# The last down projection of a two-layer trunk with Strassen's products for 8 of its 22 pairs of k-tiles

## The chip, the cores and the metric

The kernel runs on one core of one Trainium2 chip. The metric is the device time of one execution in microseconds (us), as the median over runs. The core's engines run side by side, each through its own queue in order: PE (TensorE, matrix products into PSUM banks), DVE (VectorE), ACT (ScalarE), POOL (GpSimd) and SP (SyncE, which here only issues loads and stores). An instruction that must wait holds up everything behind it in its engine's queue.

## The reference, cut to what matters

```python
for l in range(DEPTH):                     # DEPTH = 2, SEQ = 256 tokens, D_MODEL = 2048
    h = rmsnorm(x, g_mix[l])
    ...                                    # attention, spatial gating, merge
    x = x + merged @ w_out[l]
    x = x + conv_ffn(rmsnorm(x, g_ffn[l]), w_up[l], conv_w[l], conv_b[l], w_down[l])
return rmsnorm(x, g_final)

def conv_ffn(h, w_up, conv_w, conv_b, w_down):
    a, b = jnp.split(h @ w_up, 2, axis=-1)
    ...                                    # causal depthwise convolution of a
    return (jax.nn.gelu(acc) * b) @ w_down # (256 x 5632) @ (5632 x 2048)
```

All is float32. The change concerns the very last product, `(gelu(acc) * b) @ w_down[1]`, and the final norm behind it.

## The kernel before

Every float32 product with a weight matrix is made of three passes: each operand is split into two float32r parts, hi and lo, and hi\*hi, hi\*lo and lo\*hi are accumulated in PSUM. The weights arrive as tiles of two k-tiles (2 x 128 rows of the matrix) by 512 columns, `raw`, 512 KB each, loaded by SP (`fetch`, L98) into a ring of 5 buffers. `split_w` makes `hi` (ACT, L108) and `lo = raw - hi` (DVE, L109), into rings of 3 buffers each; `raw` is free for the next load when `lo` is made, and `hi` and `lo` are free when PE has used them.

In the last down projection the tokens lie on the partitions: there are NT = 2 token tiles t, FT/2 = 22 pairs m of k-tiles, and NB = 4 column blocks n of 512. The operand of pair m is `gT[m]` (two k-tiles, hi and lo, 256 tokens), in one of the 30 buffers of the `arena`. `rows` takes one column block at a time: for each of 22 pairs it loads and splits one raw tile and issues 12 matmuls of 512 columns (2 k-tiles x 2 token tiles x 3 passes; L117 to L119) into the two banks of one accumulator (`acc_banks`, ring of 3 tiles of 2 banks; two more single banks, `tp_bank`, serve the transposes). So the stage is 4 x 22 x 12 = 1056 matmuls of 512 columns. In the last column block `late=4` puts the first token tile of the last four pairs ahead of the second, so that its end runs under PE's work on the second.

Ahead of the stage the residual stream `xT` (features on partitions, 8 tiles in `xpool`) is transposed by PE through the two `tp` banks (L597, four transposes to a bank) and copied by DVE (L598) into `xb`. After each column block DVE adds the product to `xb` (L607), ACT squares and sums (L609), POOL multiplies by the gain (L611). At the end comes the norm (L613 to L619) and the four blocks are scaled and stored (L623 to L628).

The order of the instructions on each engine is set by the framework's scheduler when the program is built, which also adds the waits between engines. Nothing of it is written by hand in this stage. A tile's ring buffer is handed to the tile that comes next in that order.

Of the kernel before, what the change touches and what calls it, by code (L numbers as in the profile page):

```python
# [9 lines left out]
F32 = mybir.dt.float32  # L10
# [7 lines left out]
P = 128  # L18
# [23 lines left out]
def trunk_kernel(ctx, tc, x, g_mix, w_in, b_forget, g_sgu, w_spatial, b_spatial,  # L42
                 w_branch_a, w_branch_b, w_out, g_ffn, w_up, conv_w, conv_b,
                 w_down, g_final, out):
    """Every float32 product with a weight matrix runs as three float32r passes: each operand is
    the exact sum of two parts of 12 significant bits, hi and lo, and hi*hi + hi*lo + lo*hi
    is accumulated in PSUM. The RMS factor of a token is applied to the products, since it is
    one number per token; the gain goes into the transposed operand."""
# [95 lines left out]
    def cols_(w2d, c0, ops):  # L144
        """Products with features on the partitions, 512 features: two of [feature, f, half, token],
        where the sum of the two halves is the product."""
# [25 lines left out]
    def gained(src, gains):  # L172
        """[feature, 2, token] times a gain per feature, as an operand."""
        op = operand()
        for j in range(2):
            a = nc.scalar.activation(op[:, j, 0, :], src[:, j, :], AF.Identity, scale=gains[:, j:j + 1])
        for j in range(2):
            v = nc.vector.scalar_tensor_tensor(op[:, j, 1, :], src[:, j, :], gains[:, j:j + 1],
                                           op[:, j, 0, :].bitcast(F32), op0=ALU.mult, op1=ALU.subtract)
        return op, (a, v)  # L180
# [13 lines left out]
    def inv_rms(sq):  # L194
        """Sums of squares by feature -> [P, NT] by token, 1/sqrt(mean + eps)."""
# [9 lines left out]
    def spread(inv):  # L205
        """[P, NT] by token -> [P, 2, T], the same on every partition and twice."""
# [8 lines left out]
    def params(l):  # L215
        """Gains, conv weights and forget bias; gain() and rest() lay them out with channels on partitions."""
# [40 lines left out]
    def sgu_weights(raw):  # L257
        """The lower triangles of the spatial weights, transposed."""
# [31 lines left out]
    # ---- the first loads and products: x is transposed ahead of the chunk that needs it; until it  # L290
    # is there, products of ones keep the tensor engine's clock up ----
# [49 lines left out]
    for l in range(DEPTH):  # L341
# [191 lines left out]
        def residual(w2d, ops, sq, gains):  # L533
            """xT += w2d^T ops; its squares; its product with the gains as operands."""
# [57 lines left out]
    xb = [unit([NT, 512]) for _ in range(NB)]  # L592
    for m in range(KT // 2):
# [4 lines left out]
        nc.vector.tensor_copy(xb[m // 2][:, :, m % 2 * T:m % 2 * T + T], tp.rearrange("p (t c) -> p t c", t=NT))  # L598
    ss = small.tile([P, NT, NB], F32, tag="ss", name=nm("ss"))
    fin = small.tile([P, NT], F32, tag="fin", name=nm("fin"))  # L600
    for n in range(NB):
        gf = scratch([P, 512])
        nc.gpsimd.dma_start(gf, g_final[None, n * 512:(n + 1) * 512].broadcast_to([P, 512]))
        acc = rows(w_down[DEPTH - 1], n * 512, 512, gT, late=4 if n == NB - 1 else 0)
        for t in range(NT):
            z = xb[n][:, t, :]
            nc.vector.tensor_tensor(z, acc[t], z, op=ALU.add)  # L607
            junk = scratch([P, 512])
            nc.scalar.activation(junk, z, AF.Square, accum_out=ss[:, t, n:n + 1])  # L609
            if n < NB - 1:  # L610
                nc.gpsimd.tensor_tensor(z, z, gf, op=ALU.mult)  # L611
        if n == NB - 2:
            nc.vector.tensor_reduce(fin, ss[:, :, 0:NB - 1], axis=AX.X, op=ALU.add)  # L613
            nc.vector.tensor_scalar(fin, fin, 1.0 / D, EPS, op0=ALU.mult, op1=ALU.add)
    for t in range(NT):
        f_ = fin[:, t:t + 1]
        z = xb[NB - 1][:, t, :]
        nc.vector.scalar_tensor_tensor(f_, ss[:, t, NB - 1:NB], 1.0 / D, f_, op0=ALU.mult, op1=ALU.add)
        nc.gpsimd.tensor_tensor(f_, f_, mhalf[:, 0:1], op=ALU.pow)  # L619
        nc.vector.tensor_tensor(z, z, gf, op=ALU.mult)  # L620
# [37 lines left out]
```

## Time and profile before

| what | value |
|---|---|
| runs, median of 3 (lowest to highest) | 2717.92 us (2717.62 to 2718.63) |
| span of the profiled execution | 2717.0 us |
| median less that span, taken as what lies around it | 0.9 us |
| PE busy, DVE busy, ACT busy, POOL busy | 2702.2, 1640.7, 1304.5, 521.8 us |
| first matmul of the stage, last matmul of the program | at 2465.63 and 2707.51 us |
| share of the DMA engines' time, 2520 to 2580 us | 0.62, at 198 GB/s |

Times inside the profile count from the span's start. A row of groups gives the line of the kernel, engine, operation, the tiles (out<-in), shapes and count, then busy time in us and the mean of one in ns, then the engine's idle time before them and what ended it. A row of the timeline begins with start and length in us; for DVE the length reaches past the start of the next instruction, so the distance of starts, not the length, is the pace. "DMA to landing" runs from the issue of a load by SP to its arrival.

### The profile page before, as it was taken

What the parts mean: (1) busy time and instruction counts of PE and PEld (TensorE: products, weight loads), DVE (VectorE), ACT (ScalarE), POOL (GpSimd) and SP (SyncE); (2) the same over time, 40 slices, a digit from 0 to 9 for tenths busy, and PEclk for the clock granted to TensorE, in tenths of its full rate; (3) what the DMA queues carried; (4) which work ended last, traced back from release to release, by engine and by line L of the source; (5) the groups of instructions that cost most, each with busy time, mean ns of one, the idle gap of its engine ahead of it and who ended that gap; (6) DMA issues with size and microseconds to landing.
All of it is one profiled execution on the core that took longest, in us unless ns stands there. A gap on an engine that the chain in (4) does not pass through costs nothing.

```text
span 2717.0 us, 38197 instructions
## 1 busy us (share of the span) xinstructions
PE 2702.2 (99%) x15120; PEld 2348.1 (86%) x15120; DVE 1640.7 (60%) x1748; ACT 1304.5 (48%) x1581; POOL 521.8 (19%) x414
## 2 busy tenths in 40 slices
PE   9999999999999999999999999999999999999998
PEld 7988888888888888888889888888888888888887
DVE  5555665666666666555555556555667676766444
ACT  5454555554444444444444545555444444444443
POOL 2200113312222222100002011133122222221000
PEclk9999999999999999999999999999999999999999
DMA  7566556656666666656665655566566666665664
GB/s 233 163 198 179 170 164 186 187 187 193 182 193 184 194 180 197 204 190 190 188 185 157 201 175 173 169 188 187 190 183 188 188 189 187 188 189 190 197 198 154
DMA packets 268219, 505.13 MB, mean 186 GB/s; under 512 B 16216, under 2 KB 33032, under 8 KB 268040
## 3 DMA queue, kind: packets, MB, share of 16 engines
q1 hardware_dynamic: 267144, 500.59, 60.8%
q8 instruction: 118, 1.93, 0.3%
q0 software_dynamic: 320, 1.05, 0.1%
q10 hardware_dynamic: 576, 1.05, 0.1%
q14 instruction: 61, 0.50, 0.1%
HBM read 500.53 MB, written 2.10 MB: 185 GB/s over the span
## 4 chain that ended last, share of the span: by engine, by line
PE 97%; POOL 1%; issue 0%; DMA 0%; ACT 0%; DVE 0%; SPq 0%; POOLq 0%; ACTq 0%
PE acc L158 54%; PE acc L160 27%; PE acc L118 4%; PE acc L117 4%; PE acc L119 4%; PE tp L119 1%; PE tp L117 1%; PE tp L118 1%; POOL sq L188 0%; POOL u L170 0%; PE tp L469 0%; PE tp L490 0%; DMA u<-in_x_dram 0%; POOL tmp L420 0%; PE tp L412 0%
## 5 line engine op out<-in xcount | busy, mean ns | idle before, releaser
L158 PE MATMUL acc<-u,hi 128*128 128x512 f32 x6336 | 2206.5, 396 | 0.0
L109 DVE TENSOR_TENSOR lo<-raw,hi 128x1024 fp32r<-128x1024 f32 (+2 forms) x959 | 1239.7, 1297 | 1013.8 <-ACT hi L108 1011.6
L160 PE MATMUL acc<-u,lo 128*128 128x256 f32 x6336 | 1738.9, 280 | 0.0
L108 ACT CAST hi<-raw 128x1024 fp32r<-128x1024 f32 (+2 forms) x959 | 992.4, 1036 | 1203.5 <-PE acc L158 934.4
L158 PEld LDWEIGHTS acc<-u,hi 128*128 128x128 f32 x6336 | 1175.3, 188 | 260.8
L160 PEld LDWEIGHTS acc<-u,lo 128*128 128x128 f32 x6336 | 1193.5, 188 | 20.9 <-issue 0.4
L118 PE MATMUL acc<-lo,u 128*128 128x512 f32 (+1 forms) x584 | 217.7, 373 | 0.9 <-DVE lo L109 0.9
L117 PE MATMUL acc<-hi,u 128*128 128x512 f32 (+1 forms) x584 | 215.7, 369 | 0.0
L119 PE MATMUL acc<-hi,u 128*128 128x512 f32 (+1 forms) x584 | 215.1, 368 | 0.0
L564 POOL TENSOR_TENSOR tmp<-tmp,bc 128x512 f32<-128x512 f32 x44 | 56.4, 1281 | 376.7 <-DVE tmp L166 351.8
L118 PEld LDWEIGHTS acc<-lo,u 128*128 128x128 f32 x584 | 110.3, 189 | 16.6 <-DVE lo L109 1.5
L117 PEld LDWEIGHTS acc<-hi,u 128*128 128x128 f32 x584 | 110.3, 189 | 15.7
L119 PEld LDWEIGHTS acc<-hi,u 128*128 128x128 f32 x584 | 110.3, 189 | 15.2
L571 DVE SCALAR_TENSOR_TENSOR tmp<-tmp,cv,tmp 128x256 f32<-128x256 f32 x176 | 118.5, 721 | 0.0
L170 POOL TENSOR_TENSOR u<-tmp,u 128x512 fp32r<-128x512 f32 x68 | 110.4, 1626 | 39.5 <-ACT u L169 39.5
L188 POOL TENSOR_TENSOR sq<-sq,tmp 128x512 f32<-128x512 f32 x28 | 40.6, 1451 | 400.8 <-ACT tmp L187 399.7
L165 ACT COPY tmp<-acc 128x512 f32<-128x512 f32 x160 | 93.4, 584 | 40.0 <-PE acc L160 40.0
L166 DVE TENSOR_TENSOR tmp<-acc,tmp 128x512 f32<-128x512 f32 x160 | 109.0, 682 | 2.1 <-ACT tmp L165 0.9
L574 POOL TENSOR_TENSOR tmp<-tmp,bc 128x512 f32<-128x512 f32 x44 | 76.3, 1734 | 119.0 <-ACT tmp L573 119.0
L503 POOL TENSOR_TENSOR tmp<-tmp,bc 128x512 f32<-128x512 f32 x32 | 41.5, 1297 | 284.6 <-DVE tmp L166 284.6
L580 POOL TENSOR_TENSOR tmp<-tmp,tmp 128x512 f32<-128x512 f32 x44 | 57.0, 1296 | 190.4 <-DVE tmp L166 164.4
L169 ACT CAST u<-tmp 128x512 fp32r<-128x512 f32 x68 | 42.0, 620 | 43.6 <-POOL tmp L528 35.7
(165 smaller groups left out, 880.2 us busy)
## 6 DMA issues: line engine op xcount, KB each, us to landing
raw<-in_w_up_dram SPq DMA_DIRECT2D x352, 512.0 KB, 4.5
raw<-in_w_in_dram SPq DMA_DIRECT2D x255, 512.0 KB, 3.8
raw<-in_w_down_dram SPq DMA_DIRECT2D x176, 512.0 KB, 4.6
raw<-in_w_out_dram SPq DMA_DIRECT2D x64, 512.0 KB, 4.7
raw<-in_w_in_dram SPq DMA_DIRECT2D x48, 344.0 KB, 3.1
raw<-in_w_branch_b_dram SPq DMA_DIRECT2D x32, 512.0 KB, 4.7
raw<-in_w_branch_a_dram SPq DMA_DIRECT2D x32, 512.0 KB, 4.3
u<-in_x_dram SPq DMA_DIRECT2D x8, 256.0 KB, 7.3
```

Of the source, the lines that this page charges most:

```text
L108: a = nc.scalar.copy(hi, raw)
L109: v = nc.vector.tensor_tensor(lo, raw, hi.bitcast(F32), op=ALU.subtract)
L117: m0 = nc.tensor.matmul(o, lhsT=op[:, j, 0, ts], rhs=hi[:, jw, :], start=start, stop=False)
L118: nc.tensor.matmul(o, lhsT=op[:, j, 0, ts], rhs=lo[:, jw, :], start=False, stop=False)
L119: nc.tensor.matmul(o, lhsT=op[:, j, 1, ts], rhs=hi[:, jw, :], start=False, stop=stop)
L158: nc.tensor.matmul(acc[i][:, f, :], lhsT=hi[:, j, fs], rhs=xhl, start=k == 0, stop=False, skip_group_check=True)
L160: nc.tensor.matmul(acc[i][:, f, T:2 * T], lhsT=lo[:, j, fs], rhs=xh, start=False, stop=k == nk - 1, skip_group_check=True)
L165: nc.scalar.copy(dst, a[:, :, 1, :])
L166: nc.vector.tensor_tensor(dst, a[:, :, 0, :], dst, op=ALU.add)
L170: eng.tensor_tensor(op[:, :, 1, :], src, op[:, :, 0, :].bitcast(F32), op=ALU.subtract)
L571: nc.vector.scalar_tensor_tensor(y[:, f, :], a[:, f, tap:tap + T], cv[:, tap, ft:ft + 1], y[:, f, :], op0=ALU.mult, op1=ALU.add)
L574: nc.gpsimd.tensor_tensor(y, y, inv_b, op=ALU.mult)
```

## The change

The column blocks are now taken two at a time (g = 0, 1; q = 0, 1 inside), all eight PSUM banks are used as accumulators at once, and for 8 of the 22 pairs (m = 3, 5, ... 17) the 2 x 2 x 2 block product (2 token tiles, 2 k-tiles, 2 column blocks) is formed by 7 block products in place of 8, in Winograd's form of Strassen's algorithm. For such a pair DVE forms four sums of weight blocks (L687, L688, L692, L693), three of them in place in the two raw tiles `ra` and `rb`, and four splits follow in place of two: of `ra`, of `rb` after its sum, of `ra` after its sums, and of the half-size sum `t1` (L702 on ACT, L703 on DVE). The four sums of operand blocks are made once per pair, in g = 0 (`sums`: five additions on POOL, L610 to L614, the split on ACT L615 and DVE L616), kept in four arena buffers and in the eight `xpool` tiles, and used again in g = 1. In g = 0 the eight pairs stand at places 3, 5, ... 17 of 22, in g = 1 at places 0, 2, ... 14, each followed by a plain pair. After the last of them in a group, the products P1, R7, R6 and R5 are combined and added to `xb` (L707 to L716), beside the remaining plain pairs. P2, R3, Q4 and E are the banks of the four results (token tile, block): a plain pair adds to them (`plain`), now token tile by token tile with both blocks inside. At the end LATE = 2 pairs take the place of the four late chunks.

```diff
+    def sums(m, hi, lo):
+        z, s_ = scratch([P, 2, T]), scratch([P, 4, P])
+        nc.gpsimd.tensor_tensor(z, gT[m][:, :, 0, :].bitcast(F32), gT[m][:, :, 1, :].bitcast(F32), op=ALU.add)
+        nc.gpsimd.tensor_tensor(s_[:, 0, :], z[:, 0, P:T], z[:, 1, P:T], op=ALU.subtract)
...
+        nc.scalar.copy(hi, s_)
+        nc.vector.tensor_tensor(lo, s_, hi.bitcast(F32), op=ALU.subtract)
...
-    for n in range(NB):
-        gf = scratch([P, 512])
-        nc.gpsimd.dma_start(gf, g_final[None, n * 512:(n + 1) * 512].broadcast_to([P, 512]))
-        acc = rows(w_down[DEPTH - 1], n * 512, 512, gT, late=4 if n == NB - 1 else 0)
+    for g in range(NB // 2):
...
+        b0, b1, b2 = (acc_banks() for _ in range(3))
+        bank = {"P1": b0[:, 0], "P2": b0[:, 1], "R7": b1[:, 0], "R3": b1[:, 1], "R6": b2[:, 0], "R5": b2[:, 1],
+                "Q4": tp_bank(), "E": tp_bank()}
...
+        for i, m in enumerate(order):
+            A = left(m)
+            ra, rb = (fetch(w2d, 2 * m, 2, (n0 + q) * 512, 512) for q in range(2))
+            if i not in paired:
...
+                for t in range(1 if late else NT):
+                    plain(A, ws, t, i == NG - 1)
+                continue
...
+            t1 = scratch([P, 512])
+            nc.vector.tensor_tensor(t1, ra[:, 0, :], rb[:, 0, :], op=ALU.add)
+            nc.vector.tensor_tensor(rb[:, 0, :], rb[:, 0, :], rb[:, 1, :], op=ALU.add)
+            hi, lo = split_w(ra)
+            go("P1", A[0, 0], hi[:, 0, :], lo[:, 0, :], i == lastS)
+            go("P2", A[0, 1], hi[:, 1, :], lo[:, 1, :])
+            nc.vector.tensor_tensor(ra[:, 0, :], ra[:, 0, :], rb[:, 0, :], op=ALU.add)
+            nc.vector.tensor_tensor(ra[:, 1, :], ra[:, 1, :], ra[:, 0, :], op=ALU.add)
+            hi, lo = split_w(rb)
+            go("R7", s_[3], hi[:, 0, :], lo[:, 0, :], i == lastS)
+            go("R3", s_[4], hi[:, 1, :], lo[:, 1, :])
+            hi, lo = split_w(ra)
+            go("R6", s_[2], hi[:, 0, :], lo[:, 0, :], i == lastS)
+            go("Q4", A[1, 1], hi[:, 1, :], lo[:, 1, :])
...
+            nc.scalar.copy(hi, t1)
+            nc.vector.tensor_tensor(lo, t1, hi.bitcast(F32), op=ALU.subtract)
+            go("R5", s_[1], hi, lo, i == lastS)
```

In what follows the lines L599 to L747 are those of the changed kernel; L599 and L600 are its L597 and L598.

The first place is DVE at the start of the stage, before the change. `lo` are the splits of w_down's tiles in the order of the loads, L166 belongs to the last up projection, and the copies empty the transposes' banks.

```order
L109 TENSOR_TENSOR lo_21772<-raw_21769,hi_21771 128x1024
L166 TENSOR_TENSOR tmp_21680<-acc_21502,tmp_21680 128x512
L109 TENSOR_TENSOR lo_21790<-raw_21787,hi_21789 128x1024
L166 TENSOR_TENSOR tmp_21687<-acc_21503,tmp_21687 128x512
L109 TENSOR_TENSOR lo_21808<-raw_21805,hi_21807 128x1024
L598 COPY u_21694<-tp_21698 128x2x256
L598 COPY u_21694<-tp_21704 128x2x256
L109 TENSOR_TENSOR lo_21826<-raw_21823,hi_21825 128x1024
```

The same place now; raw_21877 and raw_21879 are the seventh and eighth loads of w_down, those of the first Strassen pair.

```order
L109 TENSOR_TENSOR lo_21810<-raw_21805,hi_21809 128x1024
L166 TENSOR_TENSOR tmp_21687<-acc_21503,tmp_21687 128x512
L687 TENSOR_TENSOR tmp_21890<-raw_21877,raw_21879 128x512
L600 COPY u_21694<-tp_21698 128x2x256
L600 COPY u_21694<-tp_21704 128x2x256
L688 TENSOR_TENSOR raw_21879<-raw_21879 128x512
L600 COPY u_21695<-tp_21710 128x2x256
L600 COPY u_21695<-tp_21716 128x2x256
L600 COPY u_21696<-tp_21722 128x2x256
L600 COPY u_21696<-tp_21728 128x2x256
L600 COPY u_21697<-tp_21734 128x2x256
L616 TENSOR_TENSOR u_21746<-tmp_21882,u_21746 128x512
```

The first sum of weights has moved ahead of all eight copies, and the copies have moved together ahead of the fourth split of w_down.

The second place is DVE inside g = 1, one Strassen pair with the plain pair that follows it in the order of places. Before the change there are only splits there, and two additions at the end of a column block:

```order
L109 TENSOR_TENSOR lo_22568<-raw_22565,hi_22567 128x1024
L109 TENSOR_TENSOR lo_22586<-raw_22583,hi_22585 128x1024
L607 TENSOR_TENSOR u_21695<-acc_22157,u_21695 128x512 x2
L109 TENSOR_TENSOR lo_22604<-raw_22601,hi_22603 128x1024
L109 TENSOR_TENSOR lo_22622<-raw_22619,hi_22621 128x1024
```

Now (raw_23044 and raw_23046 are the plain pair, raw_23080 and raw_23082 the `ra` and `rb` of the next Strassen pair, lo_23018 the split of the `rb` before):

```order
L109 TENSOR_TENSOR lo_23018<-raw_23000,hi_23017 128x1024
L109 TENSOR_TENSOR lo_23028<-raw_22998,hi_23027 128x1024
L703 TENSOR_TENSOR lo_23038<-tmp_23002,hi_23037 128x512
L687 TENSOR_TENSOR tmp_23084<-raw_23080,raw_23082 128x512
L109 TENSOR_TENSOR lo_23049<-raw_23044,hi_23048 128x1024
L688 TENSOR_TENSOR raw_23082<-raw_23082 128x512
L109 TENSOR_TENSOR lo_23053<-raw_23046,hi_23052 128x1024
L109 TENSOR_TENSOR lo_23088<-raw_23080,hi_23087 128x1024
L692 TENSOR_TENSOR raw_23080<-raw_23080,raw_23082 128x512
L693 TENSOR_TENSOR raw_23080<-raw_23080 128x512
L109 TENSOR_TENSOR lo_23100<-raw_23082,hi_23099 128x1024
```

The sum L687 of the next Strassen pair stands ahead of both splits of the plain pair before it.

The third place is PE at the start of the stage. Before, the transposes stand in twos between the products:

```order
L117 MATMUL acc_21750<-hi_21807,u_18109 128x512
L597 MATMUL tp_21710<-ident,x_84 128x128 x4
L597 MATMUL tp_21716<-ident,x_85 128x128 x4
L118 MATMUL acc_21750<-lo_21808,u_18109 128x512
L119 MATMUL acc_21750<-hi_21807,u_18109 128x512
```

Now they stand together, after the first 18 products of the stage; acc_21764 is the tile of P1 and P2, tp_21767 is Q4:

```order
L635 MATMUL acc_21764<-lo_21810,u_17711 128x512
L635 MATMUL acc_21764<-hi_21809,u_17711 128x512
L599 MATMUL tp_21710<-ident,x_84 128x128 x4
L599 MATMUL tp_21716<-ident,x_85 128x128 x4
L599 MATMUL tp_21722<-ident,x_86 128x128 x4
L599 MATMUL tp_21728<-ident,x_87 128x128 x4
L599 MATMUL tp_21734<-ident,x_88 128x128 x4
L599 MATMUL tp_21740<-ident,x_89 128x128 x4
L635 MATMUL tp_21767<-hi_21773,u_17704 128x512
```

Q4 and E lie in the transposes' two banks, so their first products come after the last transposes.

More of the change, by code (lines that the diff above doesn't have):

```diff
@@ new lines, in trunk_kernel, with three @@
+    NG = FT // 2
+    NS = 8
+    LATE = 2
+    S = []
+    for i in range(NS):
+        if i < 4:
+            u_ = unit([2, 4, P], F32R)
+            hi, lo = u_[:, 0], u_[:, 1]
+        else:
+            hi, lo = (xpool.tile([P, 4, P], F32R, tag=f"x{2 * (i - 4) + q}", name=nm("sx")) for q in range(2))
+        S.append((hi, lo))
+    of = {i: 3 + 2 * i for i in range(NS)}
+    Sx = {}
+    def three(bank, started, A, hi, lo, last):
+        for q, (l_, r_) in enumerate(((A[0], hi), (A[0], lo), (A[1], hi))):
+            nc.tensor.matmul(bank, lhsT=l_, rhs=r_, start=q == 0 and not started, stop=last and q == 2)
@@ L616, in trunk_kernel @@
         f_ = fin[:, t:t + 1]
-        z = xb[NB - 1][:, t, :]
-        nc.vector.scalar_tensor_tensor(f_, ss[:, t, NB - 1:NB], 1.0 / D, f_, op0=ALU.mult, op1=ALU.add)
+        for n in (2, 3):
+            nc.vector.scalar_tensor_tensor(f_, ss[:, t, n:n + 1], 1.0 / D, f_, op0=ALU.mult, op1=ALU.add)
         nc.gpsimd.tensor_tensor(f_, f_, mhalf[:, 0:1], op=ALU.pow)
-        nc.vector.tensor_tensor(z, z, gf, op=ALU.mult)
+        for q in range(2):
+            z = xb[2 + q][:, t, :]
+            nc.vector.tensor_tensor(z, z, gf[q], op=ALU.mult)
         for n in range(NB):
```

74 lines of the change are left out of this document (66 added, 8 removed).

## The prediction

> **What bounds the kernel now.** I read the page first, then the last 250 us by windows, by groups, by waits and by the timeline of each engine.
>
> ```profile
> PE 2702.2 (99%) x15120; PEld 2348.1 (86%) x15120; DVE 1640.7 (60%) x1748; ACT 1304.5 (48%) x1581; POOL 521.8 (19%) x414
> ...
> PE 97%; POOL 1%; issue 0%; DMA 0%; ACT 0%; DVE 0%; SPq 0%; POOLq 0%; ACTq 0%
> ```
>
> PE is the chain from end to end. A window in the stage says the same (PE, PEld, DVE, ACT, POOL busy, granted clock, DMA share, GB/s): no gap, full clock, DVE half idle.
>
> ```profile
> 2520.00:2580.00 60.00, 60.00 (x266) 49.67 (x266) 28.99 (x24) 24.44 (x26) 3.59 (x3) 1.00 0.62 198
> ```
>
> The paces, from PE's and DVE's timelines:
>
> ```profile
> 2559.95 0.39 PE L119 MATMUL acc<-hi,u 128*128 128x512 f32 x1
> 2560.63 0.39 PE L119 MATMUL acc<-hi,u 128*128 128x512 f32 x1
> 2690.20 2.36 DVE L109 TENSOR_TENSOR lo<-raw,hi 128x1024 fp32r<-128x1024 f32 x2
> 2471.37 1.27 DVE L598 COPY u<-tp 128x512 f32<-128x512 f32 x2
> 2476.13 1.03 PE L597 MATMUL tp<-ident,x 128*128 128x128 f32 x8
> ```
>
> Three matmuls lie between the first two rows: 0.227 us each. The groups below give one split 1.23 us undisturbed (1226 ns) and one copy 0.68; two follow each other in 2.36 and 1.27, so splits start 1.13 apart and half-size operations 0.59. A transpose takes 0.13. The groups from 2440 us to the end (busy us, mean ns | idle before):
>
> ```profile
> L108 ACT CAST hi<-raw 128x1024 fp32r<-128x1024 f32 x93 | 97.9, 1054 | 140.3 <-PE acc L119 106.9 <-PE tp L119 19.8 <-PE acc L158 9.6
> L598 DVE COPY u<-tp 128x512 f32<-128x512 f32 x8 | 5.1, 681 | 0.4 <-PE tp L597 0.4
> L609 ACT ACTIVATE tmp<-u 128x512 f32<-128x512 f32 x8 | 5.0, 624 | 9.9 <-DVE u L607 9.9
> L580 POOL TENSOR_TENSOR tmp<-tmp,tmp 128x512 f32<-128x512 f32 x2 | 2.6, 1293 | 9.7 <-DVE tmp L166 9.7
> L109 DVE TENSOR_TENSOR u<-raw,u 128x1024 fp32r<-128x1024 f32 x2 | 2.5, 1226 | 3.7 <-ACT u L108 3.7
> L620 DVE TENSOR_TENSOR u<-u,tmp 128x512 f32<-128x512 f32 x2 | 1.4, 690 | 0.0
> L614 DVE TENSOR_SCALAR fin<-fin 128x2 f32<-128x2 f32 x1 | 1.1, 1070 | 0.0
> ```
>
> ACT waits for PE, that is for a free `hi`: splits run three tiles ahead. L620 is the nearest row to a sum of weights: an addition of two 128x512 tiles in SBUF, 0.69 us, so 0.59 from start to start. The loads, by SP's own waits and by the line of the load from 2480 to 2690 us:
>
> ```profile
> SPq L98 <- DVE lo L109: 185.8, 82, 3.2
> DMA to landing us min/median/max: 3.6/4.5/4.9
> ```
>
> A load is issued when DVE has made a `lo` and so freed a raw tile, and lands 4.5 us later. That hides now, since five raw tiles stand 2.72 us of PE work apart.
>
> **What is removed.** 8 pairs x 2 groups x 3 matmuls = 48 of 1056 matmuls: 48 x 0.227 = 10.9 us of PE. A Strassen pair and a plain one take 45 x 0.227 = 10.2 us of PE, two plain ones 10.9. The loads stay 88 of 512 KB.
>
> **What is added to engines that are not PE.** DVE: 64 sums (0.59), 16 splits (1.13), 16 half splits L703 and 8 L616 (0.59): 70 us in a stage of 240, of which DVE leaves half idle. By busy time it fits. ACT: 16 casts of 1.05 and 24 of about 0.62, 32 us beside its 140 idle: nothing, as long as PE and DVE are not behind it. POOL: `sums` is off the path after the first two; a 128x128 addition has no row, 0.32 (a quarter of 1.3 for 128x512) to 1.0; I take 0.5, and the high end would add up to 4 us at the start (four rows of 0.5 more for each of two pairs), where ACT's L615 stands ahead of the fourth cast. The combining (L707 to L716) lies beside four or seven plain pairs. The tail after the last matmul keeps its length: the extra L735 and L739 precede the last square. What costs is the order in DVE's queue, at three places.
>
> **Place 1, the start.** Its rows: the first matmul of the stage, the eighth load of w_down, and the landings of the window 2450 to 2480 us.
>
> ```profile
> 2465.63 0.40 PE L117 MATMUL acc<-hi,u 128*128 128x512 f32 x1
> ...
> 2468.35 0.37 SPq L98 DMA_DIRECT2D raw<-in_w_down_dram  x1
> DMA to landing us min/median/max: 4.8/5.7/5.9
> ```
>
> The first L687 needs the seventh and eighth loads. The eighth is issued after the third split, as before at 2468.35, and lands at 2473.15 with 4.8 (bounds 3.6 from the stage and 5.9). DVE sits at L687 from 2468.9. PE starts the stage at 2465.63 and has 18 products, until 2469.7; the next transpose needs a copy that stands behind L687. L687 ends at 2473.8, the first copy at 2474.4, and then copy, L688, two copies in turn at 0.6; from the fifth copy on each pair waits also for PE's transposes of that pair (0.7): the seventh ends at 2479.2, and only then is Q4's bank free. PE is idle 2479.2 - 2469.7 less 24 x 0.13 of transposes that it has to make anyway: 6.4 us (5.2 to 7.5). Late next is the split of the fourth tile, which PE reaches 18 products (4.1 us) later; I count nothing for it.
>
> **Place 2, each Strassen pair after the first two.** The order in g = 1 makes a ring: when the split of `rb` ends, its raw tile goes to the next pair's `rb`; the load takes L; the next L687 waits for it; behind it in the queue stand the two splits of the plain pair, for which PE waits. From one end of `rb`'s split to the next: issue and waking 0.1, L, L687 0.59, split 1.13, L688 0.59, two splits 2.26, L692 and L693 1.18, split 1.23: 7.1 + L. PE needs 10.2. The wait per period is L - 3.1. In g = 0 one L693 goes behind the split and one L616 comes in, the same sum. L: by the stage's rows 3.6 to 4.9, median 4.5; the loads of the ring stand further apart than 2.72 us, so I take 4.3, a little under the median. 1.2 x 13 periods (7 in g = 0, 6 in g = 1) = 15.6 us; by the bounds 0.5 x 13 = 6.5 and 1.8 x 13 = 23.4.
>
> [...]
>
> In g = 0 POOL's additions run beside DVE. Two rows of DVE and POOL at the start of the stage:
>
> ```profile
> 2469.70 1.75 DVE L109 TENSOR_TENSOR lo<-raw,hi 128x1024 fp32r<-128x1024 f32 x1 [0.78 <-ACT hi L108]
> 2470.33 4.61 POOL L170 TENSOR_TENSOR u<-tmp,u 128x512 fp32r<-128x512 f32 x2
> ```
>
> Under POOL's work a split takes 1.75, not 1.23. POOL is busy 1.3 + 4 x 0.5 = 3.3 us of a period; the part of that which falls on DVE's chain I take at 1 us, at 0.4 us for each: 2.8 us for 7 periods (0 to 6).
>
> **Place 3, the change from g = 0 to g = 1.** All banks are in use, and DVE has four L724 there, then L687, L688, L692, L693, then `rb`'s split. From PE's last product of g = 0: 0.4 until the bank of E can be read, L724 0.6, L687 0.6, L688 0.8 with the small L730 between, cast of `rb` 1.05: R7 starts at 3.5, while PE has 12 products (2.7): 0.8 us. Its second product needs `lo`: 2.4 + L731 0.1 to 1.1 (its row of before is 1.07), 1.2, 1.23, so 5.0 to 5.9, against 3.8: 1.6 us. The next pair's `rb` is loaded after that split, as in place 2, with L687 and L688 both ahead of the plain split: 5.4 + 4.3 + 0.1 + 1.2 + 1.2 = 12.2, where PE, after 15 more products and the four that need `hi` alone, arrives at 9.2: 3.0 us. Together about 5.6; I take 6.0 (4 to 7).
>
> **The sum.** -10.9 + 6.4 + 15.6 + 2.8 + 6.0 = +19.9 us. On the profiled span of 2717.0 this is 2736.9; the median of the runs stands 0.9 above that span, so 2738. With all low ends -10.9 + 5.2 + 6.5 + 0 + 4 = +5 (2723), with all high ones -10.9 + 7.5 + 23.4 + 6 + 7 = +33 (2751). A measurement of this kernel tells about 0.2% (5.4 us) from no change.
>
> **The rivals.**
>
> *The loads land in time.* [...] Chance 0.11.
>
> *The clock falls.* At the program's start the windows show what idleness does to the granted clock:
>
> ```profile
> 8.00:9.00 1.00, 0.00 (x0) 0.00 (x0) 1.00 (x3) 0.79 (x2) 0.00 (x0) 1.00 1.05 381
> 9.00:10.00 1.00, 0.14 (x1) 0.14 (x2) 1.00 (x4) 0.91 (x1) 0.00 (x0) 0.58 1.05 395
> ...
> 15.00:16.00 1.00, 1.00 (x4) 0.65 (x3) 0.92 (x1) 0.00 (x0) 0.00 (x0) 0.51 1.11 398
> 16.00:17.00 1.00, 1.00 (x11) 0.92 (x9) 0.00 (x0) 0.42 (x2) 0.00 (x0) 1.00 1.03 389
> ```
>
> From 9.2 to 16 us PE ran at half clock: 6.8 us, a loss of 3.4. Place 1 holds PE for 4.7 us in one piece, and only transposes follow for 5 us more. If the clock falls there, 3.4 us are lost, of which place 2 takes back up to all, since it waits for DVE and not for PE; if it falls at place 3 too, up to 6.8: 2741 to 2745. [...] Chance 0.17.
>
> *PE's pace goes on* (the other side). DVE has half its time free, so the sums could lie in its gaps: if L687 never waited, a period would hold 8.8 us of DVE's work (the 7.1 of the ring, a split and a half split), under 10.2, and the 10.9 us would be kept: 2707, if the starts of both groups were hidden too. It decides where L falls under about 2 us, so that all waits together stay under 5.5 us. No landing here supports that. Chance 0.03.
>
> **How the numbers follow.** The forecast with its own bounds, 2738 (2723 to 2751), has 0.67; the other 0.02 is what I have not thought of. The loads in time are no change, or a loss under 2724, at 0.06 and 0.05 of their 0.11. So faster 0.04, same 0.07, slower 0.89. The range 2724 to 2752 leaves out the first and third rivals and the ends of the others.
>
> **What would show it.** Right: in g = 1 DVE idles about 1.5 us before L687 at each Strassen pair with a load as releaser, PE waits there for `lo` of the plain pair, and periods last 11.4 us; PE idles at 2470 for 4 to 5 us before a transpose; PE waits of 5 to 7 us come at the change of groups. Wrong: periods of 10.2 us (loads quick), or a wait that sits on `hi` or a bank. The prediction fails most easily by L: 0.1 us of it moves the time by 1.6 us.

## The result and the profile after

The changed kernel takes 2749.6 us (median; 2749.4 to 2750.4) against 2717.8 us (2717.6 to 2718.6) for the kernel before in the same runs: 1.0115 times as long, 95% interval 1.0102 to 1.0127. It is slower, by 31.8 us. The forecast was 2738 us with a range of 2724 to 2752: the direction and the places were right, the sizes too small, most of all at the start, in g = 0 and at the change of groups.

The page of the changed kernel: PE is still busy nearly all of the span by its busy time, but the chain of work that ended last now runs over DVE and the loads as well (before: PE 97%).

```profile
PE 2709.1 (99%) x15072; PEld 2340.2 (85%) x15072; DVE 1735.9 (63%) x1864; ACT 1334.9 (49%) x1623; POOL 568.5 (21%) x460
...
PE 91%; DVE 4%; DMA 2%; issue 1%; POOL 1%; ACT 0%; SPq 0%; POOLq 0%; DVEq 0%; ACTq 0%
```

Two windows, one in g = 0 and one in g = 1 (window, length, then PE, PEld, DVE, ACT, POOL busy, granted clock, DMA share, GB/s). Before, PE had 60.00 of 60 and DVE 28.99. Now PE has gaps, DVE works 52 of 60 us in g = 0, where POOL works too, and 46 of 58 in g = 1, where POOL does nothing:

```profile
2505.00:2565.00 60.00, 53.44 (x216) 38.89 (x216) 51.99 (x53) 30.01 (x34) 21.87 (x20) 1.00 0.53 164
2632.00:2690.00 58.00, 54.88 (x229) 41.95 (x229) 46.24 (x52) 29.99 (x32) 0.00 (x0) 1.00 0.60 185
```

The waits from 2465 to 2740 us (who waited for whom: us in total, times, longest):

```profile
DVE tmp L687 <- DMA raw<-in_w_down_dram: 18.4, 15, 4.5
...
PE acc L635 <- DVE lo L109: 10.2, 15, 1.3
...
PE acc L635 <- ACT hi L108: 7.0, 5, 5.7
...
PE tp L599 <- DVE u L600: 5.3, 1, 5.3
```

L687, the first of a pair's sums, waits 15 times for a load; PE waits for splits (15 times), for casts (5 times, the longest, 5.7, at the change of groups) and once for a copy at the start (5.3).

For a full account I took the starts of all matmuls of the stage from the trace. What lies between two starts beyond 0.227 us (0.109 for a transpose) is lost. In the kernel before that sums to 0.1 us. "Start" is the first 72 products with the transposes, "change" the last two products of g = 0 and the first 40 of g = 1. Times are medians, as difference to the kernel before in the same runs.

| kernel | start | g = 0 | change | g = 1 | lost in all | time to before |
|---|---|---|---|---|---|---|
| changed kernel | 8.9 | 15.3 | 10.2 | 7.9 | 42.3 | +31.8 |
| the prediction's terms | 6.4 | 8.4 + 2.8 | 6.0 | 7.2 | 30.8 | +20 |
| copies first | 2.5 | 17.1 | 9.9 | 6.1 | 35.7 | +24.5 |
| sums behind splits | 6.7 | 11.2 | 9.3 | 4.7 | 32.0 | +22.0 |
| gains later | 8.9 | 15.2 | 10.2 | 7.6 | 42.0 | +30.6 |
| operand sums once | 6.8 | 8.2 | 9.2 | 5.9 | 30.2 | +19.5 |
| no POOL at the change | 8.5 | 15.3 | 6.8 | 5.9 | 36.5 | +25.8 |
| plain pair first in g = 1 | 8.8 | 15.2 | 4.2 | 6.2 | 34.4 | +24.6 |
| all mended | 2.2 | 9.7 | 5.6 | 2.6 | 20.1 | +9.2 |
| wider apart | 2.2 | 1.1 | 5.9 | 2.9 | 12.1 | +4.5 |
| sums behind splits, operand sums once | 8.4 | 3.6 | 10.0 | 4.4 | 26.2 | +15.2 |
| wider apart, gains by DVE | 2.2 | 1.1 | 0.6 | 2.8 | 6.7 | -1.5 |

Less the 10.9 us of the 48 products, 42.3 leaves 31.4; the two profiled spans differ by 31.0 us and the medians by 31.8. The tail is as before: 9.53 us from the start of the last product to the end of the span, against 9.54.

### The profile page after: what moved, and what is told of

Its sections match the earlier page's. It is cut to its first block, busy times and chain, and to the rows that moved or that the text cites. A ratio compares the mean times of both kernels' runs of the same rounds, so it can differ in the third digit from the quotient of the medians.

```text
span 2748.1 us, 38349 instructions
## 1 busy us (share of the span) xinstructions
PE 2709.1 (99%) x15072; PEld 2340.2 (85%) x15072; DVE 1735.9 (63%) x1864; ACT 1334.9 (49%) x1623; POOL 568.5 (21%) x460
## 4 chain that ended last, share of the span: by engine, by line
PE 91%; DVE 4%; DMA 2%; issue 1%; POOL 1%; ACT 0%; SPq 0%; POOLq 0%; DVEq 0%; ACTq 0%
PE acc L158 54%; PE acc L160 27%; DVE lo L109 2%; DMA raw<-in_w_down_dram 2%; PE acc L118 2%; PE acc L117 2%; PE acc L119 2%; PE acc L635 2%; PE tp L635 1%; DVE raw L688 0%; POOL sq L188 0%; POOL u L170 0%; ACT hi L108 0%; DVE raw L692 0%; PE tp L469 0%
## 5 line engine op out<-in xcount | busy, mean ns | idle before, releaser
L109 DVE TENSOR_TENSOR lo<-raw,hi 128x1024 fp32r<-128x1024 f32 (+2 forms) x975 | 1267.4, 1306 | 933.5 <-ACT hi L108 930.7
L108 ACT CAST hi<-raw 128x1024 fp32r<-128x1024 f32 (+2 forms) x975 | 1007.9, 1036 | 1194.0 <-PE acc L158 934.2
L635 PE MATMUL acc<-hi,u 128*128 128x512 f32 x344 | 120.9, 401 | 6.7 <-ACT hi L108 6.6
L118 PE MATMUL acc<-lo,u 128*128 128x344 f32 (+1 forms) x320 | 114.8, 359 | 1.0 <-DVE lo L109 1.0
L117 PE MATMUL acc<-hi,u 128*128 128x344 f32 (+1 forms) x320 | 112.9, 353 | 0.0
L119 PE MATMUL acc<-hi,u 128*128 128x344 f32 (+1 forms) x320 | 112.3, 351 | 0.0
L166 DVE TENSOR_TENSOR tmp<-acc,tmp 128x512 f32<-128x512 f32 x160 | 109.0, 681 | 2.1 <-ACT tmp L165 0.9
L635 PEld LDWEIGHTS acc<-hi,u 128*128 128x128 f32 x344 | 65.6, 191 | 26.6 <-ACT hi L108 13.9
L635 PE MATMUL tp<-hi,u 128*128 128x512 f32 x248 | 87.9, 393 | 0.0
L635 PE MATMUL acc<-lo,u 128*128 128x512 f32 x172 | 69.5, 404 | 9.3 <-DVE lo L109 9.2
```

Source lines behind the costliest of these rows:

```text
L108: a = nc.scalar.copy(hi, raw)
L109: v = nc.vector.tensor_tensor(lo, raw, hi.bitcast(F32), op=ALU.subtract)
L117: m0 = nc.tensor.matmul(o, lhsT=op[:, j, 0, ts], rhs=hi[:, jw, :], start=start, stop=False)
L118: nc.tensor.matmul(o, lhsT=op[:, j, 0, ts], rhs=lo[:, jw, :], start=False, stop=False)
L119: nc.tensor.matmul(o, lhsT=op[:, j, 1, ts], rhs=hi[:, jw, :], start=False, stop=stop)
L166: nc.vector.tensor_tensor(dst, a[:, :, 0, :], dst, op=ALU.add)
```

## Experiments

All edits are to the changed kernel. Their added lines shift the numbers below them by a few (L689, L697 or L699 is L687 there, L111 is L109).

### The start: copies first

```diff
+            w1 = nc.vector.tensor_tensor(t1, ra[:, 0, :], rb[:, 0, :], op=ALU.add)
+            if g == 0 and i == 3:
+                after(w1, cp)      # cp: the last copy L600
```

> The first L687 is kept behind the last of the eight copies L600 in DVE's queue; nothing else is changed. Theory (the order in DVE's queue makes the loss at the start): the 5.47 us before the transpose at 2474.90 go, and with them the half clock from 2473.9 to 2480.7; of the 6.7 us lost there about 1 to 2 stay, since transposes and copies still take turns on two banks. 5 to 6 us faster than the changed kernel: 2743.5 to 2745. Rival (the copies and transposes set the pace by themselves, or the first L687 then comes too late and the first Strassen pair waits instead): under 2 us of gain, 2748 to 2750.

Measured: 2742.9 us, ratio to before 1.0088 (1.0075 to 1.0102), 7.3 us less above the kernel before than the changed kernel. The start loses 2.5 us in place of 8.9, so the theory holds there. In the changed kernel the timeline shows the cause (start, length, engine, line, tiles, and in brackets the idle time before and who ended it): DVE sat 4.5 us at L687, PE until the first copies were through.

```profile
2473.09 1.16 DVE L687 TENSOR_TENSOR tmp<-raw,raw 128x512 f32<-128x512 f32 x1 [4.50 <-DMA raw<-in_w_down_dram]
2474.17 1.27 DVE L600 COPY u<-tp 128x512 f32<-128x512 f32 x2
...
2474.90 1.33 PE L599 MATMUL tp<-ident,x 128*128 128x128 f32 x5 [5.30 <-DVE u L600]
```

Some of the gain went again: g = 0 loses 17.1 and not 15.3, because a half clock now follows the wait at 2494 us (1.85 us of idleness, told below). About as much came back in g = 1, which this edit does not touch: it loses 6.1 us and not 7.9 (see the run on the operand sums).

### The ring: sums behind the plain pair's splits

```diff
+        v = last_lo[0] = nc.vector.tensor_tensor(lo, raw, ...)   # L109
...
+            if i > 3 or g == 1 and i > 0:
+                after(w1, last_lo[0])                            # w1: L687
```

> Each L687 after the first of a group is kept behind the last split L109 of the plain pair ahead of it, so that the wait for the load no longer holds up the splits that PE needs. Theory (the ring through DVE's queue makes the loss per period): the load is covered by the splits of ra, t1 and of the plain pair, and DVE's chain from one split of rb to the next is 0.1 + 4.3 + 0.6 + 0.6 + 1.1 + 1.2 + 1.2 = 9.0 us, under PE's 10.2. Of the 12.2 us lost in the periods of g = 0, the 6.1 in those of g = 1 and the wait of the second pair in g = 1, at least 12 go: 2734 to 2738. Rival (DVE's and POOL's work side by side is what is too slow, and the load is not what ends it): at most the 6 us of g = 1 go, and the periods of g = 0 stay at 11.5 us or more: 2743 to 2748.

Measured: 2740.4 us, ratio 1.0080 (1.0068 to 1.0093), 9.8 us less above before: between the two expectations. In g = 1 the order in the ring set the pace. In the changed kernel five successive L687 there, of which the first and the last stand below, span 45.77 us, 11.44 a period on the mean, each after idle time that a load ended:

```profile
2642.22 0.69 DVE L687 TENSOR_TENSOR tmp<-raw,raw 128x512 f32<-128x512 f32 x1 [1.07 <-DMA raw<-in_w_down_dram]
...
2687.99 0.69 DVE L687 TENSOR_TENSOR tmp<-raw,raw 128x512 f32<-128x512 f32 x1 [1.32 <-DMA raw<-in_w_down_dram]
```

In this run they are 10.64 to 10.75 apart, none waits for a load, and PE is at work in 57.73 of 58 us:

```profile
2625.00:2683.00 58.00, 57.73 (x246) 44.98 (x245) 49.88 (x56) 30.07 (x33) 0.00 (x0) 1.00 0.62 198
```

Of the 7.9 us of g = 1 this took away 3.2, and only 1.2 to 1.4 against the runs that lose 5.9 to 6.1 there with the order unchanged. The 4.7 that stay are spread over small gaps, 0.45 us a period beyond the 10.2 of PE's work, and one wait of 0.9 at the end; their cause was not singled out. In g = 0 it took away 4.1 of 15.3 us; four of the six periods were 11.95 us, as the rival said. What holds PE there is now a cast that comes late, because DVE is: from 2490 to 2560 us ACT's casts wait 17.9 us for DVE's L692.

Another 2.2 us of the 9.8 lie at the start, which this edit does not touch. There the eighth load is issued at 2468.09 us, 2468.02 in the changed kernel, and L689 (L687) begins 3.74 us later, not 5.07:

```profile
2471.83 0.86 DVE L689 TENSOR_TENSOR tmp<-raw,raw 128x512 f32<-128x512 f32 x1 [3.16 <-DMA raw<-in_w_down_dram]
```

The half clock lasts 3.4 us there and not 6.8. Why that load lands sooner in this run no run shows.

### POOL's additions: operand sums made once

```diff
-                Sx[m] = sums(m, *S[(m - 3) // 2])
+                Sx[m] = sums(m, *S[0]) if m == 3 else Sx[3]
```

> The sums of operand blocks (five additions on POOL, a cast on ACT, a subtraction on DVE) are made for the first Strassen pair alone and used for all eight pairs; for the other seven they are left out. Theory of the prediction (POOL's additions stretch DVE's chain in g = 0): the periods of g = 0 become as those of g = 1, 11.1 us, and lose 0.8 us each where they now lose 1.6: 5 us faster, 2744 to 2746; by the size that the prediction gave, 2.8 us. Rival (what tells g = 0 from g = 1 is the order of DVE's queue, with L693 behind the split of rb): under 1.5 us of gain, 2748 to 2750.

Seven pairs thus use sums that are not theirs: this kernel leaves out work and tells only what the work costs. It leaves out POOL's additions together with the cast L615 and the split L616.

Measured: 2737.9 us, ratio 1.0074 (1.0061 to 1.0086), 12.3 us less above before, more than either theory said. In the account 7.1 us of it lie in g = 0, and these are the edit's: that is more than the theory's 5 too. The 2.1 at the start are as in the run before: L687 begins 3.80 us after the issue of the eighth load and not 5.07, and the half clock lasts one stretch of 3.4 us. The 2.0 in g = 1 also come where g = 1 is left as it is (6.1 with the copies first, 5.9 without POOL at the change): there, from the issue of a load to the L687 that waits for it, 3.6 to 3.8 us pass in this run, 3.8 to 4.4 in the changed kernel. The other 1.0 lie at the change. DVE's groups from 2490 to 2572 us (count, busy us, mean ns, idle before), first of the changed kernel:

```profile
L109 DVE TENSOR_TENSOR lo<-raw,hi 128x1024 fp32r<-128x1024 f32 x33 | 43.4, 1330 | 9.5 <-ACT hi L108 9.4
L687 DVE TENSOR_TENSOR tmp<-raw,raw 128x512 f32<-128x512 f32 x7 | 8.2, 1174 | 3.8 <-DMA raw<-in_w_down_dram 3.8
L688 DVE TENSOR_TENSOR raw<-raw 128x512 f32<-128x512 f32 x6 | 5.3, 880 | 0.0
```

and of this run:

```profile
L109 DVE TENSOR_TENSOR lo<-raw,hi 128x1024 fp32r<-128x1024 f32 x37 | 44.5, 1220 | 7.8 <-ACT hi L108 7.7
...
L687 DVE TENSOR_TENSOR tmp<-raw,raw 128x512 f32<-128x512 f32 x7 | 4.8, 693 | 8.0 <-DMA raw<-in_w_down_dram 8.0
...
L688 DVE TENSOR_TENSOR raw<-raw 128x512 f32<-128x512 f32 x7 | 4.8, 685 | 0.0
```

Beside POOL a sum takes 1.17 and 0.88 us where it takes 0.69 alone, a split 1.33 and not 1.22. Over these rows that is 33 x 0.11 + 7 x 0.48 + 6 x 0.195 = 8.2 us of DVE's time, and six L616 of 0.68 us come on top, 4.1 us. Without them the wait for the load doubles, 3.8 to 8.0 us, which takes 4.2 us back: in g = 0 the ring had been covered in part by DVE's own slowness.

### Both at once

The edits of the two runs above together.

> Both edits of the runs on the ring and on the operand sums: L687 behind the plain pair's splits, and the sums of operand blocks made for the first Strassen pair alone and used for all eight (left out for the other seven). Theory (in g = 0 the ring costs 11.3 - 10.2 us a period and POOL's additions another 1.6, and each alone leaves the other's wait or a wait for a free hi): with both gone the periods of g = 0 are those of g = 1 in the run on the ring, 10.6 to 10.8 us, and 7 x 2 = 14 us go there, 4 to 5 in g = 1, 2.5 at the start: 2728 to 2731. Rival (the two edits remove the same wait): no better than the operand sums alone in g = 0, 11.3 us, and only g = 1's 4 to 5 us come on top: 2733 to 2735.

Measured: 2733.5 us, ratio 1.0056 (1.0042 to 1.0070). In g = 0 the theory's 10.6 to 10.8 us a period came out as 10.51 (five periods between these two):

```profile
2509.45 0.69 DVE L689 TENSOR_TENSOR tmp<-raw,raw 128x512 f32<-128x512 f32 x1
...
2562.01 0.68 DVE L689 TENSOR_TENSOR tmp<-raw,raw 128x512 f32<-128x512 f32 x1
```

g = 0 loses 3.6 us: of 15.3 the ring's edit took 4.1, the operand sums' 7.1, both together 11.7. They add, so they are two causes. The total missed the theory's range by 2.5 us and lies in the rival's, though g = 0 decided against the rival. The 2.1 us that each run alone had gained at the start did not come (8.4 lost): here L689 began 5.10 us after the issue of the eighth load again, and the half clock lasted 6.8 us.

### The change of groups: gains later, no POOL, a plain pair first

In the changed kernel, DVE, POOL and PE at the change:

```profile
2607.65 1.20 DVE L687 TENSOR_TENSOR tmp<-raw,raw 128x512 f32<-128x512 f32 x1
...
2608.25 1.11 POOL L643 DMA_DIRECT2D tmp<-in_g_final_dram  x2
...
2608.88 3.53 DVE L688 TENSOR_TENSOR raw<-raw 128x512 f32<-128x512 f32 x1
2609.37 2.49 POOL L728 TENSOR_TENSOR u<-u,tmp 128x512 f32<-128x512 f32 x2
...
2613.68 0.80 PE L635 MATMUL acc<-hi,u 128*128 128x512 f32 x1 [5.74 <-ACT hi L108]
```

L688 ends at 2612.41, 0.55 us after POOL's last multiplication. The first try to take POOL away moved the lines:

```diff
-                if g == 0:
-                    nc.gpsimd.tensor_tensor(z, z, gf[q], op=ALU.mult)      # L728
...
+            if g == 1 and i == 3:
+                for t in range(NT):
+                    for q in range(2):
+                        nc.gpsimd.tensor_tensor(xb[q][:, t, :], xb[q][:, t, :], gf[q], op=ALU.mult)
+                gf = gain_rows(n0)
```

> POOL's four multiplications L728 of g = 0 and its two loads of gains L643 for g = 1 are moved out of the change of groups, to the fourth place of g = 1. Theory (POOL's work there stretches DVE's L688 from 0.69 to 3.53 us, and through it the idle time of PE and the clock): L688 takes 0.7 to 1.2 us, PE's idle time of 5.90 us falls to about 3, the half clock from 2610.7 to 2620.7 (about 2.5 us of loss) does not come: 4 to 6 us faster than the changed kernel, 2743.5 to 2745.5. Rival (L688 is long by itself at this place, or the raw tile or ACT's squares set the end): no difference, 2749 to 2750.

Measured: 2749.0 us, ratio 1.0114 (1.0100 to 1.0127): no difference to tell, 10.2 us lost at the change as before. The reason is in the trace: POOL had nothing ahead of the multiplications in its queue and made them at the same time (L681 here), and now stretched L698 (L688) and L702 (L692), where before it had held L688 alone:

```profile
2606.78 4.63 POOL L681 TENSOR_TENSOR u<-u,tmp 128x512 f32<-128x512 f32 x3 [0.79 <-ACT tmp L736]
...
2608.65 1.64 DVE L698 TENSOR_TENSOR raw<-raw 128x512 f32<-128x512 f32 x1
...
2610.32 1.64 DVE L702 TENSOR_TENSOR raw<-raw,raw 128x512 f32<-128x512 f32 x1
```

So the work was left out instead: L728 and g = 1's two L643 are gone.

> POOL's four multiplications by the gain L728 and its two loads L643 for g = 1 are left out (the first two column blocks are not multiplied by their gain, the last two use that of the first two), since moving their lines had left POOL's work where it was. Theory (POOL stretches DVE's L688 at the change of groups): L688 takes 0.7 us there, PE's idle time of 5.90 us falls to 2.5 to 3.5, the half clock does not come: of the 10.0 us lost at the change 4 to 6 go, 2743.5 to 2745.5. Rival (the four L724 and ACT's squares set the end): under 1 us of gain.

Measured: 2743.7 us, ratio 1.0094 (1.0078 to 1.0109), 6.0 us less above before. The change loses 6.8 us in place of 10.2, so 3.4 us are POOL's; 2.0 more lie in g = 1, as in other runs, so that the time fell into the theory's range by luck. L688 takes 0.69 us and PE comes back 3.9 us earlier:

```profile
2607.79 0.69 DVE L688 TENSOR_TENSOR raw<-raw 128x512 f32<-128x512 f32 x1
...
2609.74 0.50 PE L635 MATMUL acc<-hi,u 128*128 128x512 f32 x1 [2.38 <-ACT hi L108]
```

The theory missed in one point: after 2.38 and 0.90 us of waiting the half clock still came, for one stretch of 3.4 us in place of three.

The other way leaves POOL's work and begins g = 1 with a plain pair:

```diff
-            paired = {2 * i: 3 + 2 * i for i in range(NS)}
+            paired = {1 + 2 * i: 3 + 2 * i for i in range(NS)}
```

> In g = 1 the Strassen pairs stand at places 1, 3, ... 15 and not 0, 2, ... 14, so that it begins with a plain pair, whose splits can be ready before the change. Theory (the loss at the change is the time from the last product of g = 0 to the first split of a Strassen pair): PE waits under 2 us there, without a fall of the clock, and the wait of the next pair goes into the cover of the plain one: of 10.0 us 8 go, 2740.5 to 2742.5. Rival (the change costs what it costs because all banks are in use): PE waits 4 to 6 us for a bank in place of the splits, 2745 to 2749.

Measured: 2742.5 us, ratio 1.0091 (1.0077 to 1.0105), 7.2 us less above before, 6.0 of it at the change and 1.7 in g = 1; the change loses 4.2 us, where PE was to wait under 2. POOL's two multiplications (3.45 us) stretch L688 to 1.67 us, PE still waits for the cast of the Strassen pair, and the half clock comes, for 3.4 us:

```profile
2609.19 3.45 POOL L728 TENSOR_TENSOR u<-u,tmp 128x512 f32<-128x512 f32 x2
2609.82 1.67 DVE L688 TENSOR_TENSOR raw<-raw 128x512 f32<-128x512 f32 x1
...
2615.19 0.56 PE L635 MATMUL acc<-hi,u 128*128 128x512 f32 x1 [1.94 <-ACT hi L108]
```

### All mended, pairs wider apart, gains by DVE

The first of these takes copies first, sums behind splits, a plain pair first, the gains loaded and multiplied in g = 1, and:

```diff
-            hi = wspl.tile([P, 512], F32R, tag="hi", name=nm("hi"))
-            lo = wspl.tile([P, 512], F32R, tag="lo", name=nm("lo"))
+            hi, lo = (tmp.tile([P, 512], F32R, tag="tmp", name=nm("tmp")) for _ in range(2))
```

> The copies first, L687 behind the splits of the plain pair, a plain pair first in g = 1, the gains of g = 0 loaded and multiplied in g = 1, and hi and lo of t1 in buffers of tmp, so that the ring of three hi holds whole tiles alone. Theory (places 1 and 3 and the ring are orders in queues and can be had back; POOL's additions in g = 0 remain): 1 to 2 us lost at the start, 4 to 6 in the periods of g = 0, 1 to 2 at the change, 1 to 2 in g = 1, 3 in small gaps; less the 10.9 saved: 2717 to 2722. Rival 1 (the additions cost PE nothing once DVE has slack): 2711 to 2715. Rival 2 (DVE and POOL beside each other are too slow whatever the order): the periods of g = 0 stay at 11.5 us, 2724 to 2728.

Measured: 2727.1 us, ratio 1.0034 (1.0022 to 1.0047): rival 2. In g = 0 four of the periods are 12.0 us, and the change still loses 5.6.

```diff
-    NS = 8
+    NS = 6
...
-            paired = {3 + 2 * i: 3 + 2 * i for i in range(NS)}
+            paired = {3 + 3 * i: 3 + 2 * i for i in range(NS)}
```

> As the run with all places mended, but with six Strassen pairs a group, in g = 0 at places 3, 6, ... 18, so that two plain pairs stand between them and DVE and POOL have 15.6 us of PE's time for one pair's sums. 36 products are saved, 8.2 us. Theory (POOL's additions beside DVE's sums are what remains in g = 0): nothing is lost in g = 0's periods; 1 to 2 us at the start, 1 to 2 at the change, 1 in g = 1, 2 in small gaps: 2714 to 2718. Rival (each Strassen pair costs PE a wait of its own for hi or lo, whatever the distance): 1 us for each of twelve, 2722 to 2726.

Measured: 2722.3 us, ratio 1.0016 (1.0007 to 1.0025). With 15.5 to 15.9 us from pair to pair, g = 0 loses 1.1 us and not 9.7, as the theory said. The total was missed at the change, 5.9 us, and lies in the rival's range by its number alone. There POOL made its four multiplications (L683) in one run, and the half split L718 (L703) that came up 0.3 us before stood until they were done:

```profile
2590.45 5.85 DVE L718 TENSOR_TENSOR tmp<-tmp,tmp 128x512 fp32r<-128x512 f32 x1 [0.29 <-ACT tmp L717]
2590.76 4.99 POOL L683 TENSOR_TENSOR u<-u,tmp 128x512 f32<-128x512 f32 x4
```

That called for the multiplications on DVE, where one takes 0.68 us (L739 of the changed kernel), in a place with slack:

```diff
-            if g == 1 and i == 3:
+            if g == 1 and i == 14:
...
-                        nc.gpsimd.tensor_tensor(xb[q][:, t, :], xb[q][:, t, :], gf[q], op=ALU.mult)
+                        after(nc.vector.tensor_tensor(xb[q][:, t, :], xb[q][:, t, :], gf[q], op=ALU.mult), last_lo[0])
```

> As the run with the pairs wider apart, but the four multiplications of the first two blocks by their gain made by DVE, kept behind the split of place 13 in g = 1, and not by POOL. Theory (at the change POOL's four multiplications in a row held DVE's L718 for 5.85 us, and PE's 4.37 us and the half clock after it come from that): L718 takes 0.7 us, PE waits under 0.5 us at the change, the clock stays; of the 7 us lost there 6 go: 2715 to 2717, 1 to 3 us faster than the kernel before. Rival (DVE is late there by its own work, four L739 and the sums): PE still waits 2 us or more and the half clock comes: 2719 to 2722.

Measured: 2716.8 us against 2718.3, ratio 0.9995 (0.9986 to 1.0004). The change loses 0.6 us, as expected:

```profile
2590.19 0.69 DVE L718 TENSOR_TENSOR tmp<-tmp,tmp 128x512 fp32r<-128x512 f32 x1 [0.29 <-ACT tmp L717]
```

That is 33 us better than the changed kernel and level with the kernel before: 8.2 us of products saved, 6.7 lost. A gain of 1.5 us is not told from none.

One more pair:

```diff
+            paired = {**{1 + 2 * i: 3 + 2 * i for i in range(6)}, 14: 15}      # g = 1
...
-            if g == 1 and i == 14:
+            if g == 1 and i == 18:                                             # gains
```

> As the run before it (pairs wider apart, gains by DVE), with a seventh Strassen pair in g = 1 at place 14, whose operand sums are made there, three places behind the sixth; the gains go to place 18, behind the combining. Theory (three places apart a Strassen pair costs PE no wait, operand sums included): three products less, 0.7 us, and 0.5 us that the gains cost at place 14 before: 1 to 1.5 us faster than the run before it, 2715.3 to 2716, so 2 to 3 us under the kernel before. Rival (the sums at place 14 meet the end of the stage and its last squares): 0.5 to 2 us slower than the run before it, 2717.3 to 2719.

Measured: 2717.4 us against 2717.7, ratio 0.9999 (0.9990 to 1.0008). Nothing was gained; by the starts PE loses about 1.5 us at the new pair (0.57, 0.50 and 0.38 us at 2646 to 2648) and less at another place, so that g = 1 loses 0.7 us more than in the run before, as much as three products save.

## Why the prediction was right, and which terms were mis-sized

**Saved products.** 1008 products of 512 columns stand in the stage in place of 1056; 10.9 us, as predicted. The tail was rightly put at no change. That the time lies inside the range owes something to luck: the start and the change went past their high ends of 7.5 and 7, and the room for it came from the ring, whose high end of 23.4 was far from reached.

**Place 1, the start.** Mechanism right: L687 began at 2473.09, where the prediction had DVE held to 2473.15, and the copies stood behind it. That the two agree so closely is chance: the load was issued 0.3 us sooner and took 0.3 longer, and in two other runs it took 1.3 less. 8.9 us in place of 6.4 (above the 7.5 of the high end), in four parts: beside POOL L687 and L688 kept DVE 0.8 us longer than counted; transposes start 0.109 us apart and not 0.13, so that PE had 0.5 us less to do meanwhile; the stage began 0.3 us sooner; and what is left, about 0.9, is the most that the half clock, put aside as a rival, can have cost here. With the copies ahead 2.5 us are left.

**Place 2, the ring.** The predicted period was 7.1 + L = 11.4 us; in g = 1 it is 11.44 on the mean. Two errors of 0.3 us cancel in that: from the issue of the ring's load to L687 the mean is 4.1 (3.8 to 4.4), where the prediction has 4.4, its 0.1 for issue and waking included, and the rest of the round, L687 to the next issue, takes 7.3 and not 7.0 (from 2642.22 to 2649.54 us). The ring's loads have no landing of their own in the trace; the median of the stage's loads that have one is 4.2:

```profile
raw<-in_w_down_dram SPq DMA_DIRECT2D x80, 512.0 KB, 4.2
```

g = 1 lost 7.9 us, against 6 x 1.2 = 7.2. The run with the sums behind the splits took the waits for loads away, and with them 3.2 us there and 4.1 in g = 0, 7.3 us of the 15.6: the mechanism is shown, but not that the whole term was its. The rival "the loads land in time" is ruled out: with a wait of L - 3.1 a load would have to land within 3.1 us, and neither the trace before nor that of the changed kernel shows one in this stage; the shortest landing is 3.6 us in both, and the ring's loads reach L687 no sooner than 3.8 us after their issue.

**POOL beside DVE.** This is the term that was mis-sized most: "the part of that which falls on DVE's chain I take at 1 us, at 0.4 us for each: 2.8 us for 7 periods (0 to 6)". Leaving the operand sums out gained 7.1 us in g = 0, above the high end; L616, which goes with them, has a part in this that no run separates. The rate was not what failed. From 2490 to 2572 us POOL's additions for five pairs take 27.9 us in the changed kernel, 5.6 for a pair and not 3.3, since the 128x128 additions (taken at 0.5) last 0.7 to 1.2 us beside DVE:

```profile
L610 POOL TENSOR_TENSOR tmp<-u 128x512 f32<-128x512 f32 x5 | 6.5, 1301 | 41.6 <-DVE lo L703 41.6
L613 POOL TENSOR_TENSOR tmp<-tmp 128x128 f32<-128x128 f32 x5 | 6.1, 1224 | 0.0
L614 POOL TENSOR_TENSOR tmp<-tmp,tmp 128x128 f32<-128x128 f32 x5 | 6.1, 1219 | 0.4
L612 POOL TENSOR_TENSOR tmp<-tmp,tmp 128x128 f32<-128x128 f32 x5 | 5.6, 1121 | 0.0
L611 POOL TENSOR_TENSOR tmp<-tmp 128x128 f32<-128x128 f32 x5 | 3.6, 724 | 0.4
```

They run beside L687, L688 and the splits around them, and DVE loses the 8.2 us worked out above, 0.3 for each us of POOL and 1.6 for a pair, where the prediction had 0.4. One DVE instruction lost more: in the run with the pairs wider apart L718 started at 2590.45 us, 0.3 us ahead of POOL's four multiplications, and stood until they were done, 5.85 us in place of 0.69. The 0.3 us for each us in g = 0 are far from that.

**Place 3, the change.** Predicted 6.0 (4 to 7; its three parts add up to 5.4, not 5.6), found 10.2. The chain L724, L687, L688, cast was right: without POOL's work 6.8 us are lost, of which about 1.6 are the half clock (eight matmuls 0.43 apart and not 0.227). What was mis-sized was POOL again, which the prediction had not placed there at all: L688 was counted within 0.8 us and took 3.53. The 3.4 us between 10.2 and 6.8 hold both its delay and two more stretches of half clock, which followed the longer idle time, 5.74 us and not 2.38:

```profile
2610.00:2611.00 1.00, 0.00 (x0) 0.00 (x0) 1.00 (x1) 0.00 (x0) 1.00 (x2) 0.69 0.95 242
2611.00:2620.00 9.00, 5.72 (x13) 4.16 (x14) 6.71 (x9) 3.66 (x4) 0.86 (x1) 0.50 0.42 136
2620.00:2621.00 1.00, 1.00 (x5) 0.82 (x4) 1.00 (x2) 0.82 (x1) 0.00 (x0) 0.69 0.11 43
```

**The rivals.** The clock fell at both places, so the case given 0.17 is the one that came about. Its 2741 to 2745 were still too low, by 4.6 us at the least; g = 0 and g = 1 together lost 4.8 us above their terms, which that case did not touch. "PE's pace goes on" is ruled out. The sum: 2.5 + 4.1 + 4.2 + 0.7 us more than the four terms, 11.5; the span is 11.2 over the predicted 2736.9.

## What to carry to other kernels

Saving products on the bound engine did not pay here, where the work that buys it has no queue of its own: 10.9 us of PE were paid for with sums on the engine that also makes PE's operands, and three orders in its queue, with POOL beside it, cost 42, half clocks included. Before moving work to an idle engine, count the time of both as it is side by side (in g = 0 a sum L687 on DVE took 1.17 us beside POOL's additions and 0.69 without them); and put an instruction that waits for a load behind those that others wait for (7.3 us less lost in g = 0 and g = 1). Moving a line did not move its work, where the queue that it stands in was empty: the change lost 10.2 us before and after.

## What the runs showed of the hardware

**The half clock came in stretches of 3.4 us, in one place after 1.85 us of idleness.** At the change it lasted from 2610.38 to 2620.62 us by the shares of the two rows above that frame it (0.69 of a microsecond is 0.38 at full and 0.62 at half clock), 10.24 us. At the start it is 6.84 us by the same working:

```profile
2473.00:2474.00 1.00, 0.00 (x0) 0.00 (x0) 0.91 (x1) 0.00 (x0) 1.00 (x2) 0.92 0.00 0
2474.00:2480.00 6.00, 4.97 (x21) 4.11 (x22) 4.99 (x8) 1.24 (x2) 5.22 (x7) 0.50 0.01 1
2480.00:2481.00 1.00, 1.00 (x6) 0.67 (x5) 0.95 (x2) 0.00 (x0) 0.00 (x0) 0.66 0.00 0
```

With the copies first one stretch of 3.4 us follows at 2494 us, after PE had been idle for 1.85 us only (2492.22 to 2494.07):

```profile
2492.50:2494.00 1.50, 0.00 (x0) 0.00 (x0) 1.50 (x3) 0.40 (x1) 1.42 (x2) 1.00 0.11 41
2494.00:2494.50 0.50, 0.43 (x2) 0.37 (x3) 0.50 (x2) 0.00 (x0) 0.33 (x1) 0.87 0.00 0
2494.50:2497.50 3.00, 3.00 (x9) 2.33 (x8) 3.00 (x4) 0.00 (x0) 0.00 (x0) 0.50 0.74 186
2497.50:2498.00 0.50, 0.50 (x3) 0.42 (x2) 0.47 (x2) 0.00 (x0) 0.00 (x0) 0.72 0.52 152
```

By the same working this stretch is 3.41 us, and 6.84 and 10.24 are two and three of it, to 0.02. An idle time of 1.85 us was enough in one place, where waits of up to 1.3 us in g = 0 of the changed kernel were not. What decides is not settled. In the run without POOL at the change the half clock at the start begins at 2474.80 us. Of the two stretches of 3.41 us ahead of it PE worked 1.48 us in one and 0.05 in the next, and the clock stayed full in both:

```profile
2467.97:2471.38 3.41, 1.48 (x7) 0.90 (x5) 0.47 (x1) 0.62 (x1) 2.80 (x4) 1.00 0.52 163
2471.38:2474.80 3.42, 0.05 (x1) 0.05 (x1) 1.78 (x3) 0.00 (x0) 3.42 (x4) 1.00 0.03 12
```

With the copies first, PE worked 1.55 us of the 3.41 us ahead of 2494.37 us, as much, and the half clock followed at once.

**POOL's multiplications of 128x512 held DVE up, but not always in the same way.** Four multiplications in a row held one DVE instruction, L718, for 5.85 us; three in another run (gains later) let DVE's sums in between, at 1.64 us each, where one takes 0.69 alone. What decides between the two was not tried.
